# Row variance on one core: ACT takes over the waiting for loads and the reporting of groups, and enters its loop's block of code late

## The chip, the cores and the metric

The kernel runs on one core of one Trainium2 chip. The metric is device time of one execution in microseconds (us), as the median of several runs. The core's engines used here are VectorE (DVE), ScalarE (ACT), GpSimd (POOL) and SyncE (SP), which issues every DMA; TensorE (PE) has no work. Sixteen DMA engines move the data; in the trace each has a chain of packets, one after another.

## The reference

```
x: float32 [32, 512, 1024]
mean_sq = mean(x**2, axis=-1)
sq_mean = mean(x, axis=-1)**2
out     = mean_sq - sq_mean        # float32 [32, 512]
```

So for each of 16,384 rows of 1,024 numbers the kernel computes the variance. 67.11 MB are read and 0.07 MB written.

## The kernel before, in words

A row lies in one partition; 128 rows side by side are a *column* of 128 x 1024 numbers, and there are 128 columns. DVE does a column by two `BATCH_NORM_STATS2` over halves of 512 (helper `halves`, L118) and one `BATCH_NORM_AGGREGATE`. ACT does a column by two passes with accumulation: a mean (`act_mean`, L122) and a sum of squares about it (`act_var`, L127); each pass shows in the trace as an ACTIVATE and an ACTIVATION_READ_ACCUMULATOR.

**Loop part.** Columns 0 to 95 come in six groups of 16, one load of 8 MB (8.39 million bytes) each, into two buffers `xt0` and `xt1`. DVE and ACT each run a hardware loop (`Fori`) of three turns with two groups in a turn. Of a group ACT does 6 columns in batches of 3, DVE 10. Order within a group: DVE takes the semaphore `landed[b]` of the load (L215) and adds one to `go` (L216); ACT starts on `go`. DVE does its 20 half columns, waits for them (`dve_step`), does nine aggregates, waits for `act_done` from ACT, does the tenth aggregate (L225), and that one adds one to `done`. SP waits for `done` and issues the next load into the freed buffer (L98). POOL waits for `done` twice a turn and copies the results (L174); it adds one to `copied`, which DVE takes at the top of a turn.

**End part.** The last 32 columns come in eight loads of 8, 8, 5, 4, 2, 2, 1 and 1 columns (`END_LOADS`) and two pieces of half a column (`PIECES`). SP issues them as soon as the fifth `done` is there, so they queue up behind the sixth load. `END_WHO` gives each column to ACT (A) or DVE (D). The first `JOINED` = 11 columns of DVE are not aggregated by DVE: their statistics go to `stats_join`, and POOL joins them in eleven small instructions (L182 to L201). Each of DVE's nine later columns is a statistics instruction (L244), the aggregate of the column before (L253), and a statistics instruction (L248). The last column of all is DVE's, in two pieces (L260), with its aggregate at L267; the last but one is ACT's. SP stores in three parts (L105); the last, 7 columns, waits for ACT's and for DVE's last instruction.

**Where code lies.** Instructions are 64 bytes. `addr_align(..., offset=HEAD)` (L147), with HEAD = 128, stands on ACT and on DVE ahead of the first loads: each jumps, over padding, to slot 128 of a 256-slot stretch of its program and goes on from there. On both that jump shows in the trace as a COMPARE_BRANCH of L147. The runtime's code for the end of the program follows the kernel's last instruction on each engine. Code is brought in by DMA, as packets of 8,192 bytes on queue 14 (128 instructions each).

Of the kernel before, what the change touches and what calls it, by code (L numbers as in the profile page):

```python
# [11 lines left out]
def kernel(  # L12
# [14 lines left out]
    nc = tc.nc  # L27
# [4 lines left out]
    ENG = mybir.EngineType  # L32

    xf = x.flatten_outer_dims()
    N, D = xf.shape
# [9 lines left out]
    NBUF = 2  # L45
    TURNS = 3
    PER_TURN = NBUF * GROUP
    END0 = TURNS * PER_TURN
    NACT = 6
    ACT_BATCH = 3  # L50
    END_LOADS = [8, 8, 5, 4, 2, 2, 1, 1]
    END_WHO = "AADDDDDD" "AAADDDDD" "AADDD" "AADD" "DD" "AD" "D" "A"
    FIRST = END_LOADS[0] + END_LOADS[1]
    JOINED = END_WHO[:FIRST].count("D")
    PIECES = [512, 512]
    EARLY = 4
    HEAD = 128

    def sbuf(name, shape, dtype):
        return nc.alloc_sbuf_tensor(name, shape, dtype).ap()  # L60
# [8 lines left out]
    stats = sbuf("stats", [P, PER_TURN, 2, 6], FP32)  # L69
    stats_join = sbuf("stats_join", [P, JOINED, 2, 6], FP32)  # L70
    stats_end = sbuf("stats_end", [P, ncols - END0, 4, 6], FP32)
    neg_mean = sbuf("neg_mean", [P, PER_TURN], FP32)
    neg_mean_end = sbuf("neg_mean_end", [P, ncols - END0], FP32)
    two = sbuf("two", [P, JOINED, 2], FP32)
    mu = sbuf("mu", [P, JOINED, 1], FP32)
    dev = sbuf("dev", [P, JOINED, 4], FP32)
    junk = [sbuf(f"junk{i}", [P, D], mybir.dt.bfloat16) for i in range(ACT_BATCH)]
    junk_sq = [psum(f"junk_sq{i}", [P, D], FP32) for i in range(ACT_BATCH)]

    sync, act, dve, gps = nc.sync, nc.scalar, nc.vector, nc.gpsimd  # L80
    landed = [nc.alloc_semaphore(f"landed{b}") for b in range(NBUF)]
    NEND = len(END_LOADS) + len(PIECES)
    landed_end = [nc.alloc_semaphore(f"landed_end{b}") for b in range(NEND)]
    go = nc.alloc_semaphore("go")
    act_done = nc.alloc_semaphore("act_done")
    done = nc.alloc_semaphore("done")
    copied = nc.alloc_semaphore("copied")
    dve_step = nc.alloc_semaphore("dve_step")
    act_step = nc.alloc_semaphore("act_step")
    gps_step = nc.alloc_semaphore("gps_step")  # L90
    stored = nc.alloc_semaphore("stored")
    sems = [*landed, *landed_end, go, act_done, done, copied, dve_step, act_step, gps_step]

    def load(dst, c0, n, sem, f0=0, f=D):
        b0, pitch, row0 = next(b for b in BLOCKS if b[0] <= c0 < b[0] + b[1])
# [16 lines left out]
    def take(engine, sem, n):  # L112
        engine.wait_ge(sem, n)
        engine.sem_inc(sem, -n)  # L114

    def halves(st, xcol):
        for h in range(2):
            last = dve.bn_stats(out=st[:, h, :], in_=xcol[:, h * H : (h + 1) * H])  # L118
        return last

    def act_mean(i, xcol, nm):
        return act.activation(  # L122
            out=junk[i], in_=xcol, func=ACTF.Copy, scale=-S / D, accum_out=nm
        )

    def act_var(i, xcol, nm, var):
        return act.activation(  # L127
            out=junk_sq[i], in_=xcol, func=ACTF.Square, scale=S, bias=nm, accum_out=var
        )

    def end_col(c):
        k = c - END0
        return xt[0][:, k, :] if k < FIRST else xt_end[:, k - FIRST, :]
# [7 lines left out]
    early = END0 + sum(END_LOADS[:EARLY])  # L141
    act_step_of, dve_step_of = {}, {}
    joined = [c for b, c, who in end_cols if who == "D"][:JOINED]
    assert joined[-1] < END0 + FIRST and TURNS * NBUF >= NBUF + 1

    for engine in (act, dve):
        engine.addr_align(FETCH_BLOCK_INSTRUCTIONS, offset=HEAD, max_nops=0)  # L147

    with tc.tile_critical(sync_engine=ENG.Pool, no_gpsimd_drain=True):
        for g in range(NBUF):  # L150
# [21 lines left out]
    for t in range(TURNS):  # L172
# [11 lines left out]
        lambda: gps.tensor_scalar(out=mu, in0=mu, scalar1=0.25, scalar2=None, op0=ALU.mult),  # L184
        lambda: gps.tensor_tensor(out=dev, in0=mean, in1=mu.to_broadcast([P, JOINED, 4]), op=ALU.subtract),
        lambda: gps.tensor_tensor(out=dev, in0=dev, in1=dev, op=ALU.mult),
# [23 lines left out]
    gps_steps = len(steps)  # L210

    with nc.Fori(0, TURNS, engines=[ENG.DVE]):
        take(dve, copied, 1)
        for b in range(NBUF):
            take(dve, landed[b], 16)  # L215
            dve.sem_inc(go, 1)  # L216
            mine = range(b * GROUP + NACT, (b + 1) * GROUP)
            for j in mine:
                last = halves(stats[:, j, :, :], xt[b][:, j - b * GROUP, :])
            last.then_inc(dve_step, 1)  # L220
            take(dve, dve_step, 1)
            for j in mine:
                if j == mine[-1]:
                    take(dve, act_done, 1)
                last = dve.bn_aggr(out=stage[:, j, :], in_=stats[:, j, :, :])  # L225
            last.then_inc(done, 1)
    n = 0
    waiting = None
    seen = -1
    for b, c, who in end_cols:  # L230
# [6 lines left out]
        if c in joined:  # L237
            last = halves(stats_join[:, joined.index(c), :, :], col)
# [19 lines left out]
    for i, size in enumerate(PIECES):  # L258
        dve.wait_ge(landed_end[len(END_LOADS) + i], 16)
        last = dve.bn_stats(out=st[:, i, :], in_=end_col(c)[:, f : f + size])  # L260
# [7 lines left out]
    dve_steps = n + 1  # L268

    act.preload_act_table(ACTF.Square)  # L270
    with nc.Fori(0, TURNS, engines=[ENG.Activation]):
        for b in range(NBUF):
            take(act, go, 1)
            for i0 in range(0, NACT, ACT_BATCH):
                mine = range(b * GROUP + i0, b * GROUP + i0 + ACT_BATCH)
                for i, j in enumerate(mine):
                    last = act_mean(i, xt[b][:, i0 + i, :], neg_mean[:, j : j + 1])
                last.then_inc(act_step, 1)
                take(act, act_step, 1)
                for i, j in enumerate(mine):  # L280
                    last = act_var(
                        i, xt[b][:, i0 + i, :], neg_mean[:, j : j + 1], stage[:, j, 1:2]
                    )
            last.then_inc(act_done, 1)
    n = 0
    for b in range(len(END_LOADS)):
        mine = [c for bb, c, who in end_cols if bb == b and who == "A"]
# [3 lines left out]
        for i, c in enumerate(mine):  # L291
            k = c - END0
            last = act_mean(i, end_col(c), neg_mean_end[:, k : k + 1])
# [3 lines left out]
        for i, c in enumerate(mine):  # L297
            k = c - END0
            last = act_var(i, end_col(c), neg_mean_end[:, k : k + 1], mv[:, 1, c : c + 1])
# [47 lines left out]
```

## Time and profile before

| | |
|---|---|
| median of 3 runs (lowest to highest) | 163.94 us (163.92 to 164.08) |
| the profiled execution's own time | 163.92 us |
| its span, first to last instruction | 162.6 us (162.606 in the trace) |
| time around the span | 1.3 us |
| DVE busy, share of the span | 103.8 us, 64% |
| ACT busy, share of the span | 106.3 us, 65% |
| POOL busy | 3.6 us |
| DMA queue 1 (data), share of 16 engines' span | 96.4% |
| HBM read | 67.11 MB, 413 GB/s over the span |
| first load issued | 0.87 us |
| last load's landing | 159.95 us |

The span runs from the first to the last of the program's own instructions. "Busy" leaves out instructions that only wait, branch or issue. A load is split over 16 DMA engines and counts as landed when the semaphore has all sixteen increments, so each landing has sixteen times in the trace, and the last of them counts.

### The profile page before, as it was taken

To read this page: it belongs to the slowest core of one execution; us is meant where nothing else is said; L and a number is where in the kernel's file an instruction comes from. 1 tells how busy PE (TensorE), PEld (TensorE's weight loads), DVE (VectorE), ACT (ScalarE), POOL (GpSimd) and SP (SyncE) were. 2 spreads that over 40 slices of the span, in tenths; PEclk is the share of its full clock that TensorE was granted. 3 is DMA by queue.
4 is the path that set the end of the run, shared out by engine and by line. 5 is a ranking of instruction groups with operands and counts; after the bars stand their busy time and mean duration, and the time that the engine had idled before them with its cause. 6 is when DMAs were issued, how large, how long until landed. Compare 5 with 4: busy or idle time off the path is not lost. (4 is left out here: it accounts for less than half of the span.)

```text
span 162.6 us, 570 instructions
## 1 busy us (share of the span) xinstructions
DVE 103.8 (64%) x232; ACT 106.3 (65%) x189; POOL 3.6 (2%) x18
## 2 busy tenths in 40 slices
DVE  0000029980599607994099922998049979999994
ACT  3000029990599807995099932999149999799965
POOL 0000000000000000000000000000000000006000
DMA  7969979989998996996996997997989999999990
GB/s 262 516 290 484 516 322 451 516 355 419 516 419 355 516 484 290 516 500 274 516 500 274 516 516 306 468 516 339 435 387 427 468 395 417 448 416 409 414 356 7
DMA packets 2739, 67.20 MB, mean 413 GB/s; under 512 B 688, under 2 KB 688, under 8 KB 1200
## 3 DMA queue, kind: packets, MB, share of 16 engines
q1 hardware_dynamic: 2736, 67.18, 96.4%
q14 instruction: 3, 0.02, 0.1%
HBM read 67.11 MB, written 0.07 MB: 413 GB/s over the span
## 5 line engine op out<-in xcount | busy, mean ns | idle before, releaser
L118 DVE BATCH_NORM_STATS2 stats<-xt 128x6 f32<-128x512 f32 x120 | 71.8, 677 | 50.0 <-DVEq L114 50.0
L122 ACT ACTIVATE junk<-xt 128x1024 bf16<-128x1024 f32 x41 | 42.7, 1043 | 49.1 <-ACTq L114 48.0
L127 ACT ACTIVATE junk_sq<-xt,neg_mean 128x1024 f32<-128x1024 f32 x36 | 39.7, 1104 | 1.5
L118 DVE BATCH_NORM_STATS2 stats_join<-xt 128x6 f32<-128x512 f32 x22 | 13.2, 676 | 0.0
L225 DVE BATCH_NORM_AGGREGATE stage<-stats 128x2 f32<-128x12 f32 x60 | 6.0, 166 | 6.2 <-DVEq L114 5.3
L122 ACT ACTIVATION_READ_ACCUMULATOR junk<-xt 128x1 f32 x41 | 7.6, 186 | 0.0
L122 ACT ACTIVATE junk<-xt_end 128x1024 bf16<-128x1024 f32 x6 | 6.3, 1046 | 1.4 <-DMA xt_end<-in_x_dram 1.4
L127 ACT ACTIVATE junk_sq<-xt_end,neg_mean_end 128x1024 f32<-128x1024 f32 x6 | 6.7, 1110 | 0.1
L127 ACT ACTIVATION_READ_ACCUMULATOR junk_sq<-xt,neg_mean 128x1 f32 x36 | 6.7, 186 | 0.0
L244 DVE BATCH_NORM_STATS2 stats_end<-xt_end 128x6 f32<-128x512 f32 x9 | 6.1, 678 | 0.4 <-DMA xt_end<-in_x_dram 0.4
L248 DVE BATCH_NORM_STATS2 stats_end<-xt_end 128x6 f32<-128x512 f32 x9 | 5.8, 642 | 0.0
L127 ACT ACTIVATE junk_sq<-xt,neg_mean_end 128x1024 f32<-128x1024 f32 x5 | 5.5, 1105 | 0.1
L174 POOL COPY mv<-stage 128x32 f32<-128x32 f32 x3 | 0.6, 209 | 133.2 <-DVE stage L225 133.2
L270 ACT ACT_TABLE_LOAD x1 | 1.3, 1283 | 2.8 <-PEq L154 2.8
L253 DVE BATCH_NORM_AGGREGATE mv<-stats_end 128x2 f32<-128x12 f32 x9 | 1.7, 192 | 0.0
L260 DVE BATCH_NORM_STATS2 stats_end<-xt_end 128x6 f32<-128x512 f32 x2 | 1.3, 669 | 0.5 <-DMA xt_end<-in_x_dram 0.5
L127 ACT ACTIVATION_READ_ACCUMULATOR junk_sq<-xt_end,neg_mean_end 128x1 f32 x6 | 1.1, 187 | 0.0
L122 ACT ACTIVATION_READ_ACCUMULATOR junk<-xt_end 128x1 f32 x6 | 1.1, 186 | 0.0
L127 ACT ACTIVATION_READ_ACCUMULATOR junk_sq<-xt,neg_mean_end 128x1 f32 x5 | 0.9, 187 | 0.0
L182 POOL TENSOR_TENSOR two<-stats_join 128x22 f32<-128x22 f32 x1 | 0.3, 252 | 12.9 <-DVE stats_join L118 12.9
L201 POOL TENSOR_SCALAR mv<-mu 128x6 f32<-128x6 f32 (+1 forms) x2 | 0.5, 237 | 0.2
L187 POOL TENSOR_SCALAR dev<-dev 128x44 f32<-128x44 f32 x1 | 0.3, 332 | 0.1
(12 smaller groups left out, 2.3 us busy)
## 6 DMA issues: line engine op xcount, KB each, us to landing
xt<-in_x_dram SPq DMA_DIRECT2D x2, 4096.0 KB, 19.5
xt_end<-in_x_dram SPq DMA_DIRECT2D x1, 2560.0 KB, 29.8
xt_end<-in_x_dram SPq DMA_DIRECT2D x1, 2048.0 KB, 34.1
xt_end<-in_x_dram SPq DMA_DIRECT2D x2, 1024.0 KB, 37.2
xt_end<-in_x_dram SPq DMA_DIRECT2D x2, 512.0 KB, 40.4
xt_end<-in_x_dram SPq DMA_DIRECT2D x2, 256.0 KB, 40.9
xt<-in_x_dram SPq DMA_DIRECT2D x6, 24.5
out_dram<-mv SPq DMA_DIRECT2D x1, 52.5 KB, 5.3
```

The source lines that it names most:

```text
L118: last = dve.bn_stats(out=st[:, h, :], in_=xcol[:, h * H : (h + 1) * H])
L122: return act.activation(out=junk[i], in_=xcol, func=ACTF.Copy, scale=-S / D, accum_out=nm)
L127: return act.activation(out=junk_sq[i], in_=xcol, func=ACTF.Square, scale=S, bias=nm, accum_out=var)
L174: gps.tensor_copy(out=mv[:, 1, t * PER_TURN : (t + 1) * PER_TURN], in_=stage[:, :, 1]).then_inc(copied, 1)
L182: lambda: gps.tensor_tensor(out=two, in0=mean[:, :, 0:2], in1=mean[:, :, 2:4], op=ALU.add),
L201: lambda j=j, c=c, n=n: gps.tensor_scalar(out=mv[:, 1, c : c + n], in0=mu[:, j : j + n, 0], scalar1=1.0 / D, scalar2=None, op0=ALU.mult,)
L225: last = dve.bn_aggr(out=stage[:, j, :], in_=stats[:, j, :, :])
L244: dve.bn_stats(out=st[:, 0, :], in_=col[:, :H])
L248: dve.bn_stats(out=st[:, 1, :], in_=col[:, H:]).then_inc(dve_step, 1)
L253: return dve.bn_aggr(out=mv[:, :, c], in_=st)
L260: last = dve.bn_stats(out=st[:, i, :], in_=end_col(c)[:, f : f + size])
L270: act.preload_act_table(ACTF.Square)
```

## The change

1. ACT, no longer DVE, takes `landed[b]` and adds to `go`; DVE starts a group on `go`. ACT also takes `copied` at the top of a turn.
2. DVE's tenth aggregate no longer waits for ACT; it adds to `dve_done` (the new name). ACT takes `dve_done` just ahead of its last `act_var` of a group, and that one adds to `done`.
3. `JOINED` goes from 11 to 14: the three DVE columns of the third end load go to `stats_join` and POOL too (one more POOL instruction, and the others on 14 columns).
4. Only DVE is aligned ahead of the loads. ACT waits for `landed[0]`, then jumps to slot 128 directly ahead of its loop's first instruction (`head_slot`).

The static count of DVE's instructions, from the aligned slot to the kernel's last, falls from 128 to 120 (loop body 71 to 66, end part 52 to 49, five ahead of the loop in both). ACT's goes from 106 to 105: six instructions that stood behind the alignment now stand ahead of it, and the loop body goes from 56 to 61.

```diff
-    JOINED = END_WHO[:FIRST].count("D")
+    JOINED = END_WHO[: FIRST + END_LOADS[2]].count("D")
...
-    for engine in (act, dve):
-        engine.addr_align(FETCH_BLOCK_INSTRUCTIONS, offset=HEAD, max_nops=0)
+    dve.addr_align(FETCH_BLOCK_INSTRUCTIONS, offset=HEAD, max_nops=0)
...
     with nc.Fori(0, TURNS, engines=[ENG.DVE]):
-        take(dve, copied, 1)
         for b in range(NBUF):
-            take(dve, landed[b], 16)
-            dve.sem_inc(go, 1)
+            take(dve, go, 1)
             mine = range(b * GROUP + NACT, (b + 1) * GROUP)
             for j in mine:
                 last = halves(stats[:, j, :, :], xt[b][:, j - b * GROUP, :])
             last.then_inc(dve_step, 1)
             take(dve, dve_step, 1)
             for j in mine:
-                if j == mine[-1]:
-                    take(dve, act_done, 1)
                 last = dve.bn_aggr(out=stage[:, j, :], in_=stats[:, j, :, :])
-            last.then_inc(done, 1)
+            last.then_inc(dve_done, 1)
...
     act.preload_act_table(ACTF.Square)
-    with nc.Fori(0, TURNS, engines=[ENG.Activation]):
+    act.wait_ge(landed[0], 16)
+    with nc.Fori(0, TURNS, engines=[ENG.Activation], head_slot={ENG.Activation: HEAD}):
+        take(act, copied, 1)
         for b in range(NBUF):
-            take(act, go, 1)
+            take(act, landed[b], 16)
+            act.sem_inc(go, 1)
...
                 for i, j in enumerate(mine):
+                    if i0 + i == NACT - 1:
+                        take(act, dve_done, 1)
                     last = act_var(
                         i, xt[b][:, i0 + i, :], neg_mean[:, j : j + 1], stage[:, j, 1:2]
                     )
-            last.then_inc(act_done, 1)
+            last.then_inc(done, 1)
```

More of the change, by code (lines that the diff above doesn't have):

```diff
@@ L84 @@
     go = nc.alloc_semaphore("go")
-    act_done = nc.alloc_semaphore("act_done")
+    dve_done = nc.alloc_semaphore("dve_done")
     done = nc.alloc_semaphore("done")
@@ L91 @@
     stored = nc.alloc_semaphore("stored")
-    sems = [*landed, *landed_end, go, act_done, done, copied, dve_step, act_step, gps_step]
+    sems = [*landed, *landed_end, go, dve_done, done, copied, dve_step, act_step, gps_step]
     def load(dst, c0, n, sem, f0=0, f=D):
@@ L143 @@
     joined = [c for b, c, who in end_cols if who == "D"][:JOINED]
-    assert joined[-1] < END0 + FIRST and TURNS * NBUF >= NBUF + 1
-    for engine in (act, dve):
-        engine.addr_align(FETCH_BLOCK_INSTRUCTIONS, offset=HEAD, max_nops=0)
+    dve.addr_align(FETCH_BLOCK_INSTRUCTIONS, offset=HEAD, max_nops=0)
     with tc.tile_critical(sync_engine=ENG.Pool, no_gpsimd_drain=True):
```

## Prediction

> **What bounds the kernel now.** I read the page's DMA part first, then busy time by stage, then the chain that ended last.
>
> ```profile
> DMA packets 2739, 67.20 MB, mean 413 GB/s; under 512 B 688, under 2 KB 688, under 8 KB 1200
> ...
> q1 hardware_dynamic: 2736, 67.18, 96.4%
> q14 instruction: 3, 0.02, 0.1%
> ```
>
> Columns of the stages: stretch, us, DVE busy, ACT busy, POOL busy (instructions), clock, DMA share, GB/s.
>
> ```profile
> 5.00:22.00 17.00, 0.00 (x0) 0.00 (x0) 0.00 (x0) 1.00 1.01 439
> 22.00:26.00 4.00, 2.81 (x5) 2.77 (x5) 0.00 (x0) 1.00 1.06 459
> 26.00:115.00 89.00, 62.00 (x146) 63.99 (x116) 0.42 (x2) 1.00 1.01 436
> ...
> 155.00:159.00 4.00, 3.42 (x9) 2.67 (x5) 0.00 (x0) 1.00 0.84 311
> ```
>
> From 5 to 115 us the DMA share is 1.01: the 16 engines are never without data, while DVE and ACT are busy about 70% of the time. Compute in the loop is worth nothing; what counts is the slowest DMA engine's chain and what follows its last packets.
>
> The chain that ended last (start, us, what) and the last rows of the timeline:
>
> ```profile
> 117.94 40.75 DMA xt_end<-in_x_dram
> 158.70 0.02 issue
> 158.72 1.16 ACT junk L122 x2
> 159.88 0.02 issue
> 159.90 1.24 ACT junk_sq L127 x2
> ```
>
> ```profile
> 157.44 0.69 DVE L244 BATCH_NORM_STATS2 stats_end<-xt_end 128x6 f32<-128x512 f32 x1 [0.38 <-DMA xt_end<-in_x_dram]
> ...
> 158.72 1.06 ACT L122 ACTIVATE junk<-xt_end 128x1024 bf16<-128x1024 f32 x1 [1.14 <-DMA xt_end<-in_x_dram]
> 159.31 0.69 DVE L260 BATCH_NORM_STATS2 stats_end<-xt_end 128x6 f32<-128x512 f32 x1 [0.51 <-DMA xt_end<-in_x_dram]
> ...
> 160.71 0.21 DVE L267 BATCH_NORM_AGGREGATE mv<-stats_end 128x2 f32<-128x12 f32 x1
> 160.96 0.19 ACT L127 ACTIVATION_READ_ACCUMULATOR junk_sq<-xt_end,neg_mean_end 128x1 f32 x1
> ```
>
> Both engines wait for data at the end. ACT's column landed at 158.70; ACT ends at 161.14, DVE at 160.92, and the last store ends the span 1.46 after ACT.
>
> Next I read the trace's sixteen landing times of each load:
>
> ```
> load                 first   15th    last
> load 0               22.19   22.71   22.96
> load 5              118.95  119.46  119.73
> end load 5          154.35  154.87  155.13
> end load 6          155.63  156.15  157.42
> end load 7 (ACT)    156.91  157.43  158.70
> last piece (DVE)    158.21  158.76  159.95
> ```
>
> One engine is 0.25 to 0.27 behind the fifteenth from the first load on, and suddenly 1.27 behind from end load 6 on. The packet records tell why: an 8,192-byte instruction packet runs from 155.912 to 156.251, and the 4,096-byte data packets directly behind it take 0.493 and 0.482 where others take 0.16. That is 0.339 + 0.33 + 0.32 = 1.0 us on one chain, 3 us before the end, where no later work can cover it.
>
> **Whose fetch is it?** The span's two other fetches start at 1.750 (0.99 long) and 1.913 (1.02), both 0.60 after the first instruction behind a jump of L147: ACT's at 1.149, DVE's at 1.314. So an engine that enters a block has the next one fetched. The chain that begins with ACT's fetch (call it X) ends its first data packet at 5.375, DVE's (Y) at 5.589, the other fourteen between 4.908 and 5.457. Y is thus the engine that is late all along. And DVE has exactly 128 instructions from its aligned slot on, one block of 8,192 bytes: when its sequencer reads past the last, it enters the next block. ACT has 106 and stays inside.
>
> **The change, part by part.**
>
> 1. *DVE's program 8 shorter.* 128 - 5 (loop body: one `copied`, two `go`, two `act_done`) - 3 (aggregates) = 120; the kernel's last instruction moves 8 slots ahead of the border. DVE's sequencer then meets the runtime's closing code inside the block, and I take it to stop there until DVE is done. The fetch leaves the tail: Y falls back from 1.27 to 0.26 behind the fifteenth, -1.01. If instead those eight closing instructions are read ahead, the fetch stays near where it is (a rival below).
>
> 2. *ACT enters its block at 23 us.* ACT's fetch leaves 1.75 and returns about 24, on X, in the full stream of 64 KB packets (2.42 each). Without its early fetch X's first packet ends like one of the fourteen others: 0.55 to 0 ahead of their last (5.457), median 5.23, so 0.23 ahead. What a fetch between 64 KB packets costs, no row shows. Lowest: 0.34 for the packet and 0.22 for the data packet behind it (X's first took 2.64 instead of 2.42; Y's second, 2.415, lost nothing) = 0.56. The tail row gives 1.0, the early rows 1.02 + 0.24 = 1.26. Below nothing it could go only if Y, now alone in fetching early, also returned to the pack: 0.26. I take 0.8, an estimate between the tail row, the only fetch inside a running stream, and 0.56, whose following packets have the right size. X is then 0.8 - 0.23 = 0.57 behind the others' last, more than Y's 0.26, and keeps that to the end, as Y kept its 0.26. Ends: 0 and 1.26.
>
> The Trainium skill, page "Runtime: NRT & Kernel Launch", section "Instruction fetch mechanics", speaks against part 1: it calls the cost of crossing a block border one DMA tail bump, mostly hidden. By that rule nothing is won and the time stays at 163.9. This trace shows 1.0 us on one chain (and blocks of 8,192 bytes, where the page gives 16 KiB), so I go by the row.
>
> 3. *Entry, ACT first.* ACT sees `landed[0]` at 22.99, as DVE did, then a jump (ACT's took 0.43 from its start at 0.716 to the next instruction), two takes and an increment of some 0.08 each: ACT starts at 23.7 instead of 23.23, DVE 0.1 behind it. Once only.
>
> 4. *Report by ACT.* DVE's ten aggregates are done 12.93 after its first statistics (35.30 + 9 x 0.073 + 0.17 = 36.12, from 23.19). ACT's last `act_var` started 12.37 after ACT; it must now wait for `dve_done` until about 13.14, and `done` comes 14.42 after ACT's start, instead of 13.95 (37.18 - 23.23). Behind the wait stand only ACT's next group and SP's next load. Later by 0.47, and by 0.9 in the first group: `done` at 38.1. The first chain runs dry at 41.4, and a load needs 1.0 from issue to its first packet (0.868 to 1.886), so 40.4 is in time: 2.3 us of slack. Cost 0; if the slack were gone, each us late would cost one.
> After the sixth group ACT comes out 0.7 late; it waited 1.10 for the second end load (139.18), which covers that.
>
> 5. *Three more joined columns.* DVE saves 3 x 0.07 (a column takes 1.257 with its aggregate, 1.187 without): nothing, since DVE waits for data. POOL starts after 28 instead of 22 half columns, at about 150.7, and takes 3.6 + 0.35: 154.65. Its store was held by ACT until 154.98, so 0; and that store landed at 160.31, 2.2 before the end.
>
> **The sum.** The end follows ACT's last landing: 157.43 + lag + 3.91. The lag goes from 1.27 to 0.57: 162.61 - 0.70 = 161.91 span; with 1.31 around it, 163.92 - 0.70 = **163.2 us**. (The median, 163.94, is the same within 0.02.) DVE ends 0.97 after its last piece, so at 158.76 + 0.57 + 0.97 = 160.30, before ACT's 160.44.
>
> **Rivals.**
> - *Nothing gained.* Either DVE's fetch still falls before 158.7 (closing code read ahead), or ACT's fetch on X costs as much as the early rows, 1.26, with X among the last. The lag is then again about 1.27: **163.9**. For it: the costs of 1.02 at the start, and that DVE's sequencer was some 11 instructions ahead. Against: the count is exactly 128, and only one instruction beyond it set the fetch off.
> - *Slower: ACT's block is not at hand at 23 us.* ACT's jump at 0.716 found its target within 0.43, like a loop's back edge (0.35 on DVE), so it was loaded. If the later jump must fetch it, the fetch waits for a 64 KB packet (up to 2.42) plus 0.6 and 0.34 to 1.0: 3.4 to 4.0. DVE hangs on `go` as well. It decides once ACT starts after 26.0; ACT would start near 27.4, `done` at 41.8, 1.4 too late, and all engines restart (3.1 for the first packet instead of 2.42, 0.7): +2.1, less the 1.0 of part 1: **165.0**.
>
> **How the numbers follow.** Forecast 0.75 (own range 162.9 to 163.6), nothing gained 0.15, slower 0.10. The range reaches from part 2's best end (lag 0: 162.65) to the second case: 162.6 to 163.95, leaving out the slow rival and a little. A measurement here tells 0.2% (0.33 us) from no change: faster is below 163.6, slower above 164.3. Faster 0.75, same 0.15, slower 0.10.
>
> **What would show it.** Right: queue 14 with one packet near 1.9 and one at 24 to 25, none between there and 159; landings with a last engine 0.3 to 0.9 behind the fifteenth from load 1 to the end, without a jump at end load 6; ACT's first instruction near 23.7; `done` near 38.1; DMA share still 1.01 from 26 to 115. Wrong: a fetch after 150, a DMA share below 1 around 41, or a lag over 1.2.

## The result, and the profile after

The changed kernel takes 163.45 us (median of 10 runs, 163.27 to 163.63), the kernel before 163.79 us (10 runs, 163.54 to 164.08): a ratio of 0.9979, 95% interval 0.997 to 0.9988. That is 0.34 us faster, in the forecast direction and inside the range, but about half of the 0.7 forecast. The profiled execution took 163.27 us with a span of 161.571.

The same views as before. First the page's DMA lines of the changed kernel:

```profile
DMA packets 2738, 67.19 MB, mean 416 GB/s; under 512 B 688, under 2 KB 688, under 8 KB 1200
...
q1 hardware_dynamic: 2736, 67.18, 97.1%
q14 instruction: 2, 0.02, 0.0%
```

Queue 14 has lost a packet: two in the span, where before had three. The packet records put them at 1.949 (DVE's, 0.975 long) and at 26.762 (ACT's, 0.309 long). The one at 155.9 is gone. By stages (columns as in the prediction):

```profile
5.00:22.00 17.00, 0.00 (x0) 0.00 (x0) 0.00 (x0) 1.00 1.01 439
...
26.00:115.00 89.00, 61.72 (x147) 64.85 (x116) 0.42 (x2) 1.00 1.01 436
...
155.00:159.00 4.00, 3.41 (x9) 3.67 (x7) 0.00 (x0) 1.00 0.86 318
```

The stream is as full as before, 436 GB/s from 26 to 115 us, so the later `done` cost nothing. The end of the chain that ended last, and ACT's and DVE's last rows in the timeline:

```profile
118.27 39.40 DMA xt_end<-in_x_dram
157.67 0.02 issue
157.69 1.16 ACT junk L122 x2
158.85 0.02 issue
158.87 1.24 ACT junk_sq L127 x2
```

```profile
158.37 0.69 DVE L254 BATCH_NORM_STATS2 stats_end<-xt_end 128x6 f32<-128x512 f32 x1 [0.59 <-DMA xt_end<-in_x_dram]
...
159.76 0.21 DVE L261 BATCH_NORM_AGGREGATE mv<-stats_end 128x2 f32<-128x12 f32 x1
159.93 0.18 ACT L127 ACTIVATION_READ_ACCUMULATOR junk_sq<-xt_end,neg_mean_end 128x1 f32 x1
```

The same chain, 1.03 us earlier: ACT's last column starts at 157.69 instead of 158.72. The landing times say why (a load's *lag* below is its last landing minus its fifteenth):

```
changed              first   15th    last    (last of before)
load 0               22.19   22.70   22.78   22.96
load 5              119.00  119.51  119.69  119.73
end load 5          154.40  154.91  155.10  155.13
end load 6          155.68  156.19  156.38  157.42
end load 7 (ACT)    156.97  157.47  157.67  158.70
last piece (DVE)    158.31  158.81  159.00  159.95
```

Up to end load 5 the two kernels' last engines are within 0.2 us of each other; then before makes a jump and the changed kernel does not. Its last engine trails by 0.19 instead of 1.27.

Yet the profiled executions' spans differ by 1.03 us and their times by only 0.65. Around the span lay 1.31 us before; now it is 1.70. Over the ten runs of the changed kernel the time minus the span is 1.67 to 1.75; over 74 runs of before, taken beside the experiments, it is 1.26 to 1.36 (the runs' spans are recorded to 0.1 us). Some 0.4 of the gain is given back where the span does not look. That was not in the forecast, and the experiments had to find it.

### The profile page after: what moved, and what is told of

Read it like the earlier page. It is cut to its first block, busy times and chain, and to the rows that moved or that the text cites. A ratio compares the mean times of both kernels' runs of the same rounds, so it can differ in the third digit from the quotient of the medians.

```text
span 161.6 us, 568 instructions
## 1 busy us (share of the span) xinstructions
DVE 102.7 (64%) x229; ACT 106.9 (66%) x189; POOL 4.0 (2%) x19
## 5 line engine op out<-in xcount | busy, mean ns | idle before, releaser
L219 DVE BATCH_NORM_AGGREGATE stage<-stats 128x2 f32<-128x12 f32 x60 | 5.1, 161 | 0.9
L238 DVE BATCH_NORM_STATS2 stats_end<-xt_end 128x6 f32<-128x512 f32 x6 | 4.1, 683 | 0.7 <-DMA xt_end<-in_x_dram 0.7
L242 DVE BATCH_NORM_STATS2 stats_end<-xt_end 128x6 f32<-128x512 f32 x6 | 3.9, 646 | 0.0
L118 DVE BATCH_NORM_STATS2 stats_join<-xt_end 128x6 f32<-128x512 f32 x6 | 3.6, 682 | 0.0
L254 DVE BATCH_NORM_STATS2 stats_end<-xt_end 128x6 f32<-128x512 f32 x2 | 1.3, 668 | 0.6 <-DMA xt_end<-in_x_dram 0.6
L247 DVE BATCH_NORM_AGGREGATE mv<-stats_end 128x2 f32<-128x12 f32 x6 | 1.2, 194 | 0.0
L199 POOL TENSOR_SCALAR mv<-mu 128x6 f32<-128x6 f32 (+2 forms) x3 | 0.7, 236 | 0.3
```

What stands on the lines that cost most here:

```text
L199: lambda j=j, c=c, n=n: gps.tensor_scalar(out=mv[:, 1, c : c + n], in0=mu[:, j : j + n, 0], scalar1=1.0 / D, scalar2=None, op0=ALU.mult,)
L238: dve.bn_stats(out=st[:, 0, :], in_=col[:, :H])
L242: dve.bn_stats(out=st[:, 1, :], in_=col[:, H:]).then_inc(dve_step, 1)
L247: return dve.bn_aggr(out=mv[:, :, c], in_=st)
```

## The experiments

Theory A was that the gain is the code fetch that leaves the tail. Theory B gave it to DVE's lighter share and the report by ACT. Theory C, formed on the result, said that DVE's closing code costs about 0.4 us outside the span when it passes a block's border; theory D gave the gain to the late entry. "Slots" below is the room between DVE's last kernel instruction and the border of its block.

| run | slots | median us | ratio to before (95%) | median span | time minus span |
|---|---|---|---|---|---|
| changed | 8 | 163.45 | 0.9979 (0.997 to 0.9988) | 161.7 | 1.72 |
| e1_joined_only | 3 | 163.03 | 0.9957 (0.9944 to 0.997) | 161.55 | 1.50 |
| e2_act_late_only | 0 | 163.63 | 0.999 (0.9978 to 1.0001) | 162.3 | 1.32 |
| e3_act_early | 8 | 163.09 | 0.9961 (0.9944 to 0.9978) | 161.4 | 1.69 |
| e4_dve_128_again | 0 | 163.81 | 1.0005 (0.9991 to 1.0019) | 162.5 | 1.31 |
| e5_dve_slot_123 | 13 | 163.33 | 0.9977 (0.9966 to 0.9988) | 162.05 | 1.33 |
| e6_dve_slot_108 | 28 | 163.28 | 0.9976 (0.9964 to 0.9988) | 161.95 | 1.31 |
| e7_dve_127 | 1 | 163.80 | 1.0007 (0.9997 to 1.0016) | 162.5 | 1.32 |
| e8_fetch_at_144 | passed early | 163.74 | 1.0009 (0.9999 to 1.0018) | 162.4 | 1.32 |
| e9_dve_114 | 14 | 162.78 | 0.9945 (0.9931 to 0.9959) | 161.5 | 1.33 |
| e10_no_swap | 3 | 163.18 | 0.9973 (0.9959 to 0.9987) | 161.6 | 1.60 |
| e11_changed_again | 8 | 163.36 | 0.9978 (0.9968 to 0.9989) | 161.65 | 1.69 |

The groups e1 to e4, e5 to e8 and e9 to e11 ran on three chips, each group with before beside it, so between groups the ratios compare and not the times.

### One part alone: e1_joined_only

```diff
 (before)
-    JOINED = END_WHO[:FIRST].count("D")
+    JOINED = END_WHO[: FIRST + END_LOADS[2]].count("D")
...
-    assert joined[-1] < END0 + FIRST and TURNS * NBUF >= NBUF + 1
```

> The kernel before, with three more joined columns alone: DVE's program from the aligned slot is 125 instructions long instead of 128; who waits for loads, who reports groups and ACT's early jump stay as before. Theory A (the gain is the code fetch that leaves the tail, about 1.0 us of one DMA engine's chain): no packet on queue 14 between 3 and 158 us, the last engine 0 to 0.3 behind the fifteenth at end load 7, span near 161.6, time about 163.4, as the changed kernel or a little below. Theory B (the gain is DVE's lighter share and the report by ACT, the fetch is beside the point): the fetch may go, but the time stays within 0.1 of the 163.8 of before. Theory C (what the tail wins is partly lost around the span): the time minus the span is 1.7, as in the changed kernel, where the profiled execution of before had 1.3.

One line of the change, alone, wins 0.8 us, more than twice the whole change. Against the changed kernel 0.2 of that lie outside the span (1.50 instead of 1.72) and 0.15 in the median span. Its page and the last rows of its chain:

```profile
q14 instruction: 2, 0.02, 0.1%
```

```profile
157.67 0.02 issue
157.69 1.16 ACT junk L122 x2
```

No code packet starts between 2 and 162 us; the lag at end load 7 is 0.16. A holds, B falls. The time minus span is 1.40 to 1.72, and here the trace shows a piece of it: a code packet at 162.92, and the clearing of semaphores 156 to 206 after the program, which starts 0.33 us after the span's end in before, starts 0.87 after it; the four other engines' blocks of semaphores keep their times. By its change with DVE's program length I take that block for DVE's.

### One part alone: e2_act_late_only

```diff
 (before)
-    for engine in (act, dve):
-        engine.addr_align(FETCH_BLOCK_INSTRUCTIONS, offset=HEAD, max_nops=0)
+    dve.addr_align(FETCH_BLOCK_INSTRUCTIONS, offset=HEAD, max_nops=0)
...
-    with nc.Fori(0, TURNS, engines=[ENG.Activation]):
+    act.wait_ge(go, 1)
+    with nc.Fori(0, TURNS, engines=[ENG.Activation], head_slot={ENG.Activation: HEAD}):
```

> The kernel before, with ACT's jump to its block moved to the first load's arrival (it waits for go there) and nothing else. Theory A: two things happen that don't add up, because they sit on different chains: the fetch near 155.9 stays, with its 1.0 us on DVE's engine, and ACT's fetch comes at 24 to 27 with about 0.57 on ACT's engine, which stays behind the other. Lag about 1.2 at end load 7, time 163.6 to 164.0, the same as before. If the late entry itself cost anything on the path, the time would rise over 164.1. Theory C: time minus span 1.3.

No difference from before that the interval can tell (0.9978 to 1.0001). Both fetches are in the trace, at 27.05 and 155.96; the tail's, on the other chain, hides the first.

### Undoing one part: e3_act_early

```diff
 (changed)
-    dve.addr_align(FETCH_BLOCK_INSTRUCTIONS, offset=HEAD, max_nops=0)
+    for engine in (act, dve):
+        engine.addr_align(FETCH_BLOCK_INSTRUCTIONS, offset=HEAD, max_nops=0)
...
-    act.wait_ge(landed[0], 16)
-    with nc.Fori(0, TURNS, engines=[ENG.Activation], head_slot={ENG.Activation: HEAD}):
+    with nc.Fori(0, TURNS, engines=[ENG.Activation]):
```

> The changed kernel, with ACT aligned ahead of the loads again, as before, and no wait ahead of its loop: everything else as changed. Theory A: queue 14 has its two packets near 1.8 and 1.9 and none in the stream; lag 0 to 0.3 at end load 7; time 163.2 to 163.5, so within 0.2 of the changed kernel's 163.45: the late entry is worth nothing or a little less than nothing. If the late entry is the gain (theory D), the time is back at 163.8. Theory C: time minus span 1.7.

Without the late entry the change would have won 0.74 us instead of 0.34. The lag at end load 7 is 0.05, and the chain ends earlier still:

```profile
157.48 0.02 issue
157.50 1.16 ACT junk L122 x2
158.66 0.02 issue
158.69 1.24 ACT junk_sq L127 x2
```

ACT starts its last column at 157.50, 0.19 ahead of the changed kernel; the medians of the spans are 0.3 apart. D falls: without the late entry the gain is still there. By the medians the late entry is a cost, and a larger one than the 163.2 to 163.5 expected here allowed for, though the intervals of the two ratios overlap. The gap of 1.69 shows that C's 0.4 does not come from ACT.

### Giving the fetch back: e4_dve_128_again

```diff
 (changed; spare is a new semaphore that nothing waits for)
+    for _ in range(8):
+        dve.sem_inc(spare, 1)
     with nc.Fori(0, TURNS, engines=[ENG.DVE]):
```

> The changed kernel, with eight increments of an unused semaphore ahead of DVE's loop, so that its program is 128 instructions long again; they run at 2.8 us, twenty us before DVE has work. Theory A: a fetch is back at 155 to 156, the last engine is about 1.2 behind the fifteenth from end load 6 on, the span is back near 162.5 and the time at 163.8 or above, 0.35 to 1.0 over the changed kernel. Theory B: the time stays at 163.45. Theory C: time minus span is 1.3 again.

Eight instructions that run 20 us before DVE has work undo the whole gain: 163.81 us, ratio to before 1.0005. Its page and the end of its chain:

```profile
q14 instruction: 3, 0.02, 0.1%
```

```profile
159.04 0.02 issue
159.06 1.16 ACT junk L123 x2
160.22 0.02 issue
160.25 1.24 ACT junk_sq L128 x2
```

The third code packet is back, at 155.51, with data packets of 0.50 and 0.49 behind it, and the last engine trails by 1.34 at end load 7. (This execution, 164.27 us, is at the upper end of its kernel's runs; the median span is 162.5.) And the time minus span is back at 1.31. The same eight slots bring both.

### How many slots: e7_dve_127, e5_dve_slot_123 and e6_dve_slot_108

```diff
 (before: e7)
-    JOINED = END_WHO[:FIRST].count("D")
+    JOINED = END_WHO[:FIRST].count("D") + 1
...
-    assert joined[-1] < END0 + FIRST and TURNS * NBUF >= NBUF + 1
 (e3_act_early: e5; e6 has HEAD - 20)
-    for engine in (act, dve):
-        engine.addr_align(FETCH_BLOCK_INSTRUCTIONS, offset=HEAD, max_nops=0)
+    for engine, slot in ((act, HEAD), (dve, HEAD - 5)):
+        engine.addr_align(FETCH_BLOCK_INSTRUCTIONS, offset=slot, max_nops=0)
```

> The kernel before, with one more joined column (12 instead of 11): one aggregate fewer, so DVE's program is 127 instructions long. Theory A as recorded: DVE's sequencer passes the border only behind its 128th instruction and stops at the closing code until DVE is done, so one instruction less is enough: no fetch between 3 and 158 us, lag under 0.3 at end load 7, span near 161.5. If the sequencer reads on into the closing code, the fetch stays near 156 and the span near 162.5. Theory C: time minus span 1.4 to 1.7 in the first case, 1.3 in the second.

One instruction less is enough to keep the fetch out of the loads: the lag at end load 7 is 0.01, the smallest of all runs. But the time is that of before. The waits of SP, which issues the last store and waits for it, say where it went; before first, then e7 (line, cause, us in all, times, longest):

```profile
SPq L316 <- DMA out_dram<-mv: 1.0, 1, 1.0
```

```profile
SPq L311 <- DVE mv L266: 4.7, 1, 4.7
SPq L315 <- DMA out_dram<-mv: 1.9, 1, 1.9
```

DVE finishes at 159.9, the closing code follows, and the fetch comes at 161.06, on top of the last store: fifteen engines finish that store by 161.47, the sixteenth at 162.41. So my step "one instruction beyond sets it off" was right, and the expectation drawn from it, that one less is enough, was wrong in the time: the fetch moved from the last loads to the last store. It lies inside the span there, so the 1.4 to 1.7 that theory C gave for the time minus the span was not met either: it is 1.32.

> The changed kernel with ACT's early jump back (as in e3_act_early), and DVE's jump to slot 123 instead of 128: the five instructions ahead of DVE's loop end one block and the loop begins the next, so that the runtime's closing code begins 13 slots ahead of the border instead of 8. Theory C (DVE's closing code, when it passes a block's border after the kernel's last instruction, adds about 0.4 us outside the span): if the closing code fits into the 13 slots, time minus span goes from 1.7 to 1.3; if it is longer, it stays between 1.4 and 1.7. If C is wrong and the length of the program itself makes the 1.7, it stays at 1.7 too, and only a gap of 1.3 tells. DVE's fetch now comes when its loop begins, near 3.4 to 5 us and inside the stream, so about 0.57 on DVE's engine: span 161.4 to 161.8. Time 162.9 to 163.4.

> As e5_dve_slot_123, but slot 108: 28 slots between the kernel's last instruction and the border, and the border now runs through DVE's loop, fifteen instructions into the body. Theory C: time minus span is 1.3, if 28 slots hold the closing code. Theory A on fetches: one near 27 us when DVE first passes the border, inside the stream; if each turn's way back to the block before needs it fetched anew, two or three more, each about 0.57 on the same chain, so lag up to 1.5 and span up to 162.9; if the blocks stay loaded, one alone, span 161.4 to 161.8 and a time of 162.7 to 163.1, the best so far.

With 13 and with 28 slots the time minus span is 1.33 and 1.31: C holds, and by it the closing code up to the program's end needs more than 8 and at most 13 slots. What these two win there they lose on the fetch, which falls into the stream: at 7.86 us in e5, 0.31 long with a data packet of 2.95 behind it (0.84 in all), at 29.2 in e6, 0.31 and 2.97 (0.86). The 0.57 expected was 0.27 and 0.29 too little, which fits median spans 0.25 and 0.15 above the 161.4 to 161.8 expected. In e6 DVE's way back over the border fetched nothing again.

### Moving the fetch: e8_fetch_at_144

```diff
 (before)
-    for engine in (act, dve):
-        engine.addr_align(FETCH_BLOCK_INSTRUCTIONS, offset=HEAD, max_nops=0)
+    for engine, slot in ((act, HEAD), (dve, HEAD + 24)):
+        engine.addr_align(FETCH_BLOCK_INSTRUCTIONS, offset=slot, max_nops=0)
```

> The kernel before, with DVE's jump to slot 152 instead of 128, nothing else: the border is passed 24 instructions earlier, so the fetch that came at 155.9 comes near 143 to 145, when the data packets are 16 KB (0.61 us each) and not 4 KB (0.16). Theory A: the fetch costs its own 0.3 plus 0.25 to 0.65 on the packets behind it, on DVE's chain, and this lag stays to the end: 0.6 to 1.2 at end load 7. If two packets pay (as among 4 KB), span near 162.4 and time 163.6 to 163.9; if one pays 0.26 (as among 64 KB), span near 162.0 and time near 163.3 to 163.5. Theory C: time minus span 1.3, since the closing code lies wholly in a block that DVE entered long before.

The fetch came at 138.5, earlier than expected, and the time is as before. The packet records give its size: 0.309 for the packet, and 1.289 for the 20 KB data packet behind it where others take 0.761, so 0.84 in all; the packet after that took 0.762 again. One packet paid, and yet the time is the one expected if two pay. The lag went only from 0.30 to 0.52, below the 0.6 expected, because the engine with the fetch had been the eleventh of sixteen, 0.47 ahead of the last. The fifteenth landing now is that of the engine which had been last, by 0.30, since the first load.

### The swap, and all of it together: e10_no_swap, e9_dve_114, e11_changed_again

```diff
 (e2_act_late_only: e10)
-    JOINED = END_WHO[:FIRST].count("D")
+    JOINED = END_WHO[: FIRST + END_LOADS[2]].count("D")
...
-    assert joined[-1] < END0 + FIRST and TURNS * NBUF >= NBUF + 1
 (e3_act_early: e9)
-    JOINED = END_WHO[: FIRST + END_LOADS[2]].count("D")
+    JOINED = END_WHO[: FIRST + END_LOADS[2] + END_LOADS[3]].count("D")
...
-            take(dve, go, 1)
+            dve.wait_ge(go, 1)
...
                 last = halves(stats[:, j, :, :], xt[b][:, j - b * GROUP, :])
+                if j == mine[0]:
+                    last.then_inc(go, -1)
             last.then_inc(dve_step, 1)
-            take(dve, dve_step, 1)
+            dve.wait_ge(dve_step, 1)
             for j in mine:
                 last = dve.bn_aggr(out=stage[:, j, :], in_=stats[:, j, :, :])
+                if j == mine[1]:
+                    last.then_inc(dve_step, -1)
```

> The kernel before, with the three more joined columns and ACT's late jump, but without the swap: DVE waits for loads and reports groups (ACT waits for go ahead of its jump). DVE has 125 instructions. Theory A: the swap is worth nothing by itself and the late jump costs about 0.35 on ACT's chain: time 163.3 to 163.5, span about 161.8, that is e1_joined_only plus 0.35. If the late jump only costs where ACT leads (an interaction with the swap), the time is near 163.05, as in e1_joined_only.

e10 came out at 163.18, 0.15 over e1 in time and between its two expectations; by ratio the late entry costs 0.0016 here (0.9957 to 0.9973) and 0.0018 between e3 and the changed kernel (0.9961 to 0.9979), about 0.3 us each, though the intervals overlap in both pairs, and in e10 some 0.1 of it lies outside the span (1.60 instead of 1.50). That the late entry costs something is thus likely and its size in the time is not shown; what its fetch costs one engine is (0.57 to 0.59, below). In e10's profiled execution the fetch does not show in the lag (0.04). The swap by itself cannot be told from nothing: 0.9973 without it, 0.9978 with it (e11), on the same chip, with median spans of 161.6 and 161.65.

> As e3_act_early (the changed kernel with ACT's early jump back), with DVE's program cut from 120 to 114 instructions: two more joined columns, and the two takes of a group done by instructions that are there anyway. The closing code begins 14 slots ahead of the border, one more than in e5_dve_slot_123, where the time outside the span was 1.3. Theories A and C together: no fetch between 3 us and the end, lag under 0.2, span near 161.4 as in e3_act_early, time minus span 1.3, time 162.6 to 162.8: 1.0 under before, the whole of what the fetch cost. If C is wrong, time minus span is 1.7 and the time 163.0 to 163.1.

e9 is the fastest: 162.78 us, 0.9 under before (163.69) and 0.6 under the changed kernel on the same chip. Its page and the end of its chain:

```profile
span 161.4 us, 555 instructions
...
q14 instruction: 2, 0.02, 0.0%
```

```profile
157.51 0.02 issue
157.54 1.16 ACT junk L122 x2
158.69 0.02 issue
158.72 1.24 ACT junk_sq L127 x2
```

Both code packets lie at 1.77 and 1.90, the lag at end load 7 is 0.02, and the time minus span is 1.33. So A and C each have their price, and both prices can be avoided at once.

> The changed kernel itself, for a comparison on the same chip with e9_dve_114 and e10_no_swap: 163.4 to 163.5, time minus span 1.7.

It took 163.36 us.

## Why the prediction was half right, point by point

- **What bounds the kernel: right.** DMA share 1.01 from 26 to 115 us in every run, and in each run with a fetch in the tail the last engine's lag is what moves ACT's last column.
- **The count of 128: right.** 128 instructions bring the fetch (before, e2, e4), 127, 125 and 120 do not bring it into the loads. What failed is a side step. DVE's sequencer does seem to "stop there until DVE is done" (e7's fetch comes 1.17 after DVE's last instruction), but then it goes on through the closing code and passes the border. The price comes there: 0.9 us on the last store with 1 slot, 0.2 to 0.3 outside the span with 3, 0.4 with 8, nothing with 13 or more. With 1 and with 3 slots the trace shows the code packet; with 8 it is inferred.
- **The tail's price: right.** Forecast -1.01 of lag; the two profiled executions gave 1.27 to 0.19. e1, which removes the fetch alone, took 0.95 off the median span.
- **The late entry's price: right sign, too large.** I took 0.8 for the fetch; the trace has 0.309 for the packet and 2.68 instead of 2.42 behind it, 0.57, the low end of my range. The four further fetches of ACT among 64 KB packets (e2, e4, e10, e11) took 0.58 to 0.59, DVE's two 0.84 and 0.86. X's lag was 0.19 (0.25 in e11), not 0.57: 0.23 of the difference is the fetch, the other 0.15 that X's first packet had ended early, at 5.03, which the median of the engines taken for it could not foresee. The fetch also came later than the forecast "24 to 25": it starts at 26.76, as the data packet of 24.35 to 26.77 ends.
- **The step that failed: "with 1.31 around it".** The sum took the time outside the span over from before as a constant. It measured 1.72. The forecast span was 161.91 and the measured median 161.7, lower by 0.2; the time missed by 0.25 the other way, the difference being these 0.4. That the time lies so near the forecast is in part luck: an error of 0.2 in the span stood against one of 0.4 outside it. The own rival ("closing code read ahead") looked at the same code but asked only whether its fetch would fall into the loads.
- **The forecast's base** was the profiled execution's 163.92, which lies above the medians of before seen since, 163.65 to 163.83. Against the 163.79 of the result that is another 0.13 of the gain that was not there.
- **Costs put at nothing: right.** ACT's jump took 0.43 (22.865 to 23.298), so its block was at hand and the slow rival is out; ACT began at 23.55 (forecast 23.7), SP issued load 2 at 37.97 (`done` forecast near 38.1). ACT's new wait is in the waits of the changed kernel:

```profile
ACT junk_sq L127 <- ACTq L114: 4.1, 6, 0.7
```

Six times 0.7, as worked out (13.14 - 12.37), and without effect: SP's issue at 37.97 still leaves 2.4 us.

On the Trainium skill's sentence that crossing a block border is mostly hidden ("Runtime: NRT & Kernel Launch", "Instruction fetch mechanics"): here the measurements decide against it. Crossing in the last 4 us of the loads cost 0.26% of the time, some 0.4 us, net of what it saved at the close (e4 against the changed kernel: 1.0005 and 0.9979 of before).

**What stays open.** How the 0.4 us arises in the closing code with 8 slots: the trace ends before it, and only in e1 and e10 (3 slots) does a late clearing of semaphores show. That the room behind DVE's code in its block decides it is shown (e4, e5, e6, e9); the mechanism is argued. Also open is what slows single 64 KB packets in some executions (2.5 to 3.2 us, most of them near 41, 61 and 80 us).

## What to carry to other kernels

When a kernel is bound by a full DMA stream, find the last engine's lag in the sixteen landing times of each load, and look at the packet records where it jumps: a code fetch of 8 KB is paid by one engine and by everybody who waits for the whole load. Count the instructions of each engine up to the next block border, leave room for the code that runs after the kernel as well, and take the unavoidable fetches before the stream is under way. And when a change touches the end of a program, compare times and not spans: check that the time outside the span has stayed.

## What the runs showed of the hardware that was not expected

- A fetch of 8,192 bytes costs the engine that carries it 0.57 to 0.86 us among 64 KB packets and 0.84 among 20 KB packets (e8), where one data packet behind it is slowed, and about 1.0 among 4 KB packets, where two are. In the stream it starts as a data packet of its engine ends (26.76 in the changed kernel, 138.51 in e8). What it costs the load depends on where its engine stands: 0.84 moved the last landing by 0.52 in e8. With all fetches at 1.7 to 2.2 us, before the stream is under way, the lag at the first load was 0.01 to 0.41.
- Delays on different engines did not add up here: e2, with a fetch on each of two chains, is no slower than before.
- A code packet at the wrong moment holds up a 3.5 KB store: the wait for it went from 1.0 to 1.9 us in e7.
- A loop that spans a block border (e6) was fetched once, not once a turn.
